# Where a split operand waits for its place: T4's slot lent to a weight, and six reloads of the output moved ahead

## The chip, the core and the metric

One core of a Trainium2 chip runs the kernel. The metric is device time in microseconds of one execution, the median of several; 902.73 us for the kernel before (three runs, 902.01 to 903.17).

## The reference, cut to what matters

The layer puts 16 learned tokens ahead of a sequence of 2048, normalises it, projects it once to eight groups of 512 columns, runs a gated short convolution on four groups and a chunked retention with four heads on the other four, and projects the concatenated result back, with a residual and a last normalisation.

```python
hn = rms_norm(h, norm_g)
proj = jnp.einsum('bld,de->ble', hn, w_in)
cx, cb, cc, cg, q, k, v, rg = jnp.split(proj, 8, axis=-1)
conv_out = short_conv_branch(cx, cb, cc, conv_w) * jax.nn.silu(cg)
qf = rotary(q.reshape(shp), pos) * (RET_HEAD_DIM ** -0.5)
kf = rotary(k.reshape(shp), pos)
ret = head_group_norm(retention_chunkwise(qf, kf, vf), ret_norm_g)
mixed = jnp.concatenate([conv_out, ret * jax.nn.silu(rg)], axis=-1)
return rms_norm(h + jnp.einsum('ble,ed->bld', mixed, w_out), final_g)
```

## The kernel before, in words

Every large product is done in single precision by three passes: `split` (L103, L111) cuts an operand into a high part (an ACT cast) and a low part (a subtraction, on VectorE by default), and TensorE multiplies low by high, high by low and high by high. An operand of 512 columns (the moving side, `mh` and `ml`) stays in a slot of its own, `mh{i}{kt}` for operand i and row block kt; `operand` (L139) gives operand 7 the slot of operand 4.

Two ways of multiplying share these operands. `quad` (L199, matmuls at L208) is Strassen and Winograd's scheme: a 2 x 2 block product by seven products instead of eight, with operands 0 to 6 of the moving side, where 0, 1 and 5 are blocks, and 2, 3, 4 and 6 the sums T2, T1, T3 and T4. `quad_plain` (L247, matmuls at L258) multiplies the four blocks themselves, operands 0, 7, 1 and 5, and needs none of the sums; its weights are split into a slot of the moving side that is not yet in use (`plain_parts`, slots `FIRST_W` and `PLAIN_W`). It is used where the sums are not there yet: twice for the first head of the first half of the rows (`r == 0`), once for the second half, once for the first pair of the output.

The rows are worked in two halves, `r`. In each, four retention heads (`head`) come first, then four convolution groups (`conv_group`). At the front of the first half `moving` loads and splits the blocks of x; `block_sums` makes the sums (T1 in `t1`, T3 in `t3`, T2 in `b22`, T4 in `b21`); T2 and T4 are split at once, and T1 and T3 in `rest()`, after the second plain quad, because `PLAIN_W` is T1's slot. For the second half and for the output weights the sums are made ahead by `prepare` and stored in DRAM (`sums_x`, `sums_w`); `prepared` loads them through tiles of the pool `g` (16 tiles of 512 columns) and splits them. In the output, `output(0, ...)` loads T2 and T4 ahead of its plain quad and T1 and T3 after it; `output(1, ...)` is the first Strassen quad there.

Of a retention head, these names matter: `kv` and `qg` hold the rotated keys, values and queries, `pm` the masked scores (VectorE, L603), read by the matmuls L611, next to L612, which read the states; L573 and L578 are transposes of keys and values, L588 the state matmuls, L601 the scores. After `pm` the output of a head is normalised over its columns (statistics L617 and L619, GpSimd's power L624, VectorE's L628) and transposed (L635).

The order in which each engine issues is set by a scheduler at build time, which simulates the program; the kernel's text gives dependencies and priorities. So an edit of the text moves instructions elsewhere. All loads and stores are issued from SP, in one queue.

Of the kernel before, what the change touches and what calls it, by code (L numbers as in the profile page):

```python
# [14 lines left out]
P = 128  # L15
# [4 lines left out]
NG = 4  # L20
# [9 lines left out]
HIGH = 400  # L30
BRIEF = 2
BLOCK = ((0, 7), (1, 5))
FIRST_W, PLAIN_W, B12 = 2, 3, 4
SUMS = (3, 2, 4, 6)


# [32 lines left out]
def hybrid_trunk(ctx: ExitStack, tc: tile.TileContext, t, out: bass.AP, chunk_decay):  # L69
# [20 lines left out]
    def gen(name="g"):  # L90
        return sb.tile([P, HB + 16], F32, name=name, tag="g", bufs=GEN)[:, : 2 + HB]
# [96 lines left out]
                nc.sync.dma_start(dst[n, kt], a)  # L188
            yield

    def prepared(m, src, ns):

        for n in ns:
            for kt in range(KH):
                a = gen("t")[:, :HB]
                nc.sync.dma_start(a, src[n, kt])
                parts(m, SUMS[n], kt, a)

    def quad(w, m, take):  # L199
# [43 lines left out]
    def plain_parts(loads, slot=PLAIN_W):  # L243
        w = {n: plain_part(n, loads[n], slot)[1] for n in (0, 2, 1, 3)}
        return [w[n] for n in range(4)]
# [398 lines left out]
    def output(pair, m, final_g):  # L644
        d = mixed[pair // 2]
        loads = [
            lambda a, i=i, k=k: nc.sync.dma_start(a.rearrange("p (k c) -> p k c", k=KH), d[pair % 2, i, k])
            for i in range(2)
            for k in range(2)
        ]  # L650
        ys = [[None, None], [None, None]]
        ss = small.tile([P, 2, 2], F32, name="so", tag="so")
        for i in range(2):
            for j in range(2):
                y = gen("yo")[:, :HB]
                row = (2 * pair + i) * P
                nc.sync.dma_start(y, x[row : row + P, j * HB : (j + 1) * HB])
                ys[i][j] = y
        last = [None]

        def take(i, j, pp, c):
            y = ys[i][j]
            if c is not None:
                add(nc.gpsimd, y, y, c)
            last[0] = nc.vector.tensor_tensor(out=y, in0=pp, in1=y, op=ALU.add)  # L665
            junk = sb.tile([P, HB], F32, name="rot", tag="rot", bufs=1)
            nc.scalar.activation(junk, y, AF.Square, accum_out=ss[:, i, j : j + 1])
            if i == j:
                ys[i][j] = gen("z")[:, :HB]
                nc.gpsimd.tensor_tensor(out=ys[i][j], in0=y, in1=final_g[:, j * HB : (j + 1) * HB], op=ALU.mult)  # L670

        if pair == 0:
            w = plain_parts(loads)
            prepared(m, sums_w, (1, 3))
            quad_plain(w, m, take)
            prepared(m, sums_w, (0, 2))
        else:
            quad(stationary(load_raw(loads)), m, take)
        for i in range(2):
            tot = small.tile([P, 1], F32, name="tot", tag="tot")  # L680
            add(nc.vector, tot, ss[:, i, 0:1], ss[:, i, 1:2])
            rs = small.tile([P, 1], F32, name="rf", tag="rf")
            rsqrt_mean(rs, tot)
            row = (2 * pair + i) * P
            for j in range(2):
                cs = slice(j * HB, (j + 1) * HB)
                y = ys[i][j]
                if i == j:
                    nc.scalar.mul(y, y, rs)
                else:  # L690
                    with tc.issue_after(last[0].ins):
                        nc.vector.scalar_tensor_tensor(
                            out=y, in0=y, scalar=rs, in1=final_g[:, cs], op0=ALU.mult, op1=ALU.mult
                        )
                nc.sync.dma_start(out[row : row + P, cs], y)
# [24 lines left out]
    warm_up(WARM)  # L720
    nc.sync.dma_start(gain, t["norm1_g"])
    factors = [[] for _ in range(NR)]
    for r in range(NR):
        f = factors[r]
        rot_t = sb.tile([P, 2, BLK], F32, name="rot_t", tag="rot_t", bufs=1)
        p0 = NMETA + r * BLK

        def load_tables():
            nc.sync.dma_start(rot_t, t["rot"][:, :, p0 : p0 + BLK])

        if r == 0:
            w = [None] * 4
            loads = w_loads(0)

            def begin(half):
                for n in (half, 2 + half):
                    w[n] = plain_part(n, loads[n], FIRST_W)

            m, b = moving(
                load_x(r), gain_of, {(0, 0): lambda: begin(0), (0, KH - 1): lambda: begin(1), (0, KT - 1): normalise_meta}  # L740
            )
            first = [[p for a, p in w]]
            blocks = None, meta_products([a for a, p in w])
            first.append(plain_parts(w_loads(1)))
            load_tables()
            nc.sync.dma_start(cols, t["cols"])
            t3 = [a[:, i * HB : (i + 1) * HB] for a in (row_tile("t3") for _ in range(2)) for i in range(2)]
            t1 = [brief("t1") if n < BRIEF else sb.tile([P, HB], F32, name="t1", tag="tc", bufs=COPIES) for n in range(KH)]
            for kt in range(KH):
                b11, b21, b12, b22 = (b[n * KH + kt] for n in range(4))  # L750
                block_sums(b11, b12, b22, b21, t1[kt], t3[kt], gain_of(kt), gain_of(KH + kt), nc.gpsimd)
                parts(m, 2, kt, b22)
                parts(m, 6, kt, b21)
            for _ in row_factors(0, f):
                pass
            nc.sync.dma_start(causal, t["causal"])
            nc.sync.dma_start(conv_w, t["conv_w"])
            nc.sync.dma_start(ret_g, t["ret_norm_g"])

            def rest():  # L760
                for i, held in ((3, t1), (4, t3)):
                    for kt in range(KH):
                        parts(m, i, kt, held[kt])

            between = (lambda: None, rest)
            later = prepare(load_x(1), sums_x, gain_of)
        else:
            m, b = moving(load_x(r), gain_of)
            first = [plain_parts(w_loads(0))]
            load_tables()  # L770
            prepared(m, sums_x, (1, 3))
            between = (lambda: prepared(m, sums_x, (0, 2)),)
            blocks = None, None
            later = prepare(load_w_out, sums_w)
        for h in range(NG):
            blocks = head(h, r, m, rot_t, f, blocks, lambda: ahead(r, h + 1), *((first, between) if h == 0 else ()))
            if h > 0:
                next(later, None)
                next(later, None)
        steps = row_factors(r + 1, factors[r + 1]) if r < NR - 1 else iter(())  # L780
        for g in range(NG):
            blocks = conv_group(g, r, m, f, blocks, lambda: ahead(r, NG + g + 1))
            for _ in range(3):
                next(steps, None)
# [44 lines left out]
```

## Time and profile before

| what | value |
|---|---|
| median of three runs | 902.73 us (902.01 to 903.17) |
| the profiled execution | 903.85 us |
| its span on the core | 902.1 us |
| mean granted TensorE clock | 0.994 |
| TensorE busy | 885.0 us, 98% |
| VectorE busy | 714.6 us, 79% |
| ACT busy | 406.1 us, 45% |
| GpSimd busy | 398.9 us, 44% |
| DMA | 116.94 MB, mean 130 GB/s |

The page is of one execution. Its span leaves out 1.75 us around the program's instructions. A TensorE that is busy for 98% need not be at its pace: matmuls overlap, and their ends are modelled, so the distance from start to start tells more than the busy time. The clock is given as a share of 2.4 GHz; 0.50 is 1.2 GHz.

### The profile page before, as it was taken

The page shows a single profiled execution, that of the slowest core. Times are in us where ns is not written, and L with a number is a line of the kernel's source. Part 1 is how long each engine was busy: PE and PEld are TensorE (multiplying, and loading weights), DVE is VectorE, ACT ScalarE, POOL GpSimd, SP SyncE. Part 2 cuts the span into 40 slices and gives each one's busy share as a digit, 9 for nine tenths or more (in the row PEclk, how much of TensorE's full clock was granted, in tenths as well). Part 3 has the DMA queues.
Part 4 walks back from the last instruction along what each step waited for, and adds up shares of the span by engine and source line. Part 5 has one row for each costly group of instructions (what it writes and reads, how often), then busy time and mean ns, then how long its engine had stood idle before and what let it go on. Part 6 is the DMA issues. An engine that isn't in the chain of part 4 may idle for free.

```text
span 902.1 us, 12862 instructions
## 1 busy us (share of the span) xinstructions
PE 885.0 (98%) x4407; PEld 727.8 (81%) x4407; DVE 714.6 (79%) x1173; ACT 406.1 (45%) x815; POOL 398.9 (44%) x294
## 2 busy tenths in 40 slices
PE   8998999999999999999999999999999999999996
PEld 5787888888878777788888888888888878788885
DVE  6798888897686776899889899777667697866764
ACT  8771342424344443655333332433333465554553
POOL 0533132323355554461333323345546445777763
PEclk9998999999999999999999999999999999999999
DMA  9711352623234232744125262113231685555532
GB/s 333 239 40 38 104 195 59 205 82 107 79 103 127 78 108 78 253 180 141 38 73 203 73 236 68 50 56 90 57 88 48 210 280 178 162 186 152 182 111 93
DMA packets 76242, 116.94 MB, mean 130 GB/s; under 512 B 7632, under 2 KB 24336, under 8 KB 76176
## 3 DMA queue, kind: packets, MB, share of 16 engines
q1 hardware_dynamic: 76176, 116.11, 40.1%
q8 instruction: 35, 0.57, 0.3%
q14 instruction: 31, 0.25, 0.1%
HBM read 90.92 MB, written 25.17 MB: 129 GB/s over the span
## 4 chain that ended last, share of the span: by engine, by line
PE 83%; DVE 9%; DMA 3%; ACT 2%; issue 2%; POOL 1%; SPq 0%; POOLq 0%; DVEq 0%; ACTq 0%
PE pj L208 66%; PE pj L258 7%; DVE ml L111 2%; DVE wl L111 2%; PE ms L611 2%; PE ms L612 1%; PE ms L601 1%; PE ms L588 1%; PE ms L392 1%; DVE rot L513 1%; DMA ra<-in_w_in 1%; PE ms L635 1%; PE ms L573 1%; DVE rot L512 1%; PE ms L578 1%
## 5 line engine op out<-in xcount | busy, mean ns | idle before, releaser
L208 PE MATMUL pj<-mh,wl 128*128 128x512 f32 x1008 | 400.0, 397 | 1.0 <-ACT tc L215 0.8
L208 PE MATMUL pj<-ml,wh 128*128 128x512 f32 x1008 | 394.2, 391 | 1.1 <-DVE ml L111 1.1
L208 PE MATMUL pj<-mh,wh 128*128 128x512 f32 x1008 | 393.4, 390 | 0.0
L99 ACT CAST wh<-ra 128x512 fp32r<-128x512 f32 x216 | 133.8, 620 | 315.1 <-PE pj L208 272.4
L208 PEld LDWEIGHTS pj<-mh,wl 128*128 128x128 f32 x1008 | 189.6, 188 | 43.1 <-ACT tc L215 2.2
L208 PEld LDWEIGHTS pj<-ml,wh 128*128 128x128 f32 x1008 | 189.8, 188 | 39.6 <-DVE ml L111 1.9
L208 PEld LDWEIGHTS pj<-mh,wh 128*128 128x128 f32 x1008 | 189.6, 188 | 39.8
L111 DVE TENSOR_TENSOR wl<-ra,wh 128x512 fp32r<-128x512 f32 x216 | 192.4, 892 | 36.2 <-ACT wh L99 35.2
L111 POOL TENSOR_TENSOR ra<-ra 128x512 f32<-128x512 f32 x72 | 113.0, 1570 | 82.0 <-DVE qg L556 32.3
L108 POOL TENSOR_TENSOR sa<-ra 128x512 f32<-128x512 f32 x36 | 54.9, 1525 | 122.6 <-DVE wl L111 62.1
L111 POOL TENSOR_TENSOR ra<-sa,ra 128x512 f32<-128x512 f32 x36 | 52.2, 1450 | 98.3 <-DVE wl L111 98.0
L215 ACT COPY tc<-pj 128x512 f32<-128x512 f32 x108 | 62.6, 580 | 0.0
L258 PE MATMUL pj<-ml,mh 128*128 128x512 f32 x128 | 50.8, 396 | 0.1
L258 PE MATMUL pj<-mh,mh 128*128 128x512 f32 x128 | 50.2, 395 | 0.0
L258 PE MATMUL pj<-mh,ml 128*128 128x512 f32 x128 | 48.5, 396 | 1.5 <-DVE ml L111 1.5
L624 POOL TENSOR_TENSOR rp<-rs,neg_half 128x4 f32<-128x4 f32 x16 | 19.9, 1245 | 51.0 <-DVE rs L108 50.8
L466 POOL TENSOR_TENSOR c<-c,rr 128x512 f32<-128x512 f32 x16 | 30.0, 1874 | 24.0 <-DVE c L454 13.6
L108 DVE TENSOR_TENSOR tc<-pj,tc 128x512 f32<-128x512 f32 x32 | 22.0, 688 | 23.4 <-PE pj L208 23.4
L111 DVE TENSOR_TENSOR ml<-t,mh 128x512 fp32r<-128x512 f32 x40 | 36.6, 961 | 0.8 <-ACT mh L99 0.8
L99 ACT CAST wh<-sa 128x512 fp32r<-128x512 f32 x36 | 22.3, 620 | 32.7 <-PE pj L208 32.7
L665 DVE TENSOR_TENSOR yo<-pj,yo 128x512 f32<-128x512 f32 x32 | 22.0, 688 | 18.8 <-POOL yo L108 8.9
L466 POOL TENSOR_TENSOR c<-c,tc 128x512 f32<-128x512 f32 x16 | 27.3, 1706 | 19.0 <-ACT tc L492 17.6
(128 smaller groups left out, 1134.3 us busy)
## 6 DMA issues: line engine op xcount, KB each, us to landing
ra<-in_w_in SPq DMA_DIRECT2D x128, 256.0 KB, 2.7
x<-in_xT SPq DMA_DIRECT2D x48, 256.0 KB, 5.1
w<-in_w_out SPq DMA_DIRECT2D x32, 256.0 KB, 5.0
ra<-mixed SPq DMA_DIRECT2D x32, 256.0 KB, 2.7
yo<-in_x SPq DMA_DIRECT2D x32, 256.0 KB, 4.4
ra<-in_x SPq DMA_DIRECT2D x16, 256.0 KB, 3.7
mixed<-qg SPq DMA_DIRECT2D x16, 256.0 KB, 2.3
sums_x<-x SPq DMA_DIRECT2D x16, 256.0 KB, 2.4
```

The costliest lines, as they stand in the source:

```text
L99: nc.scalar.copy(out=hi, in_=src)
L108: eng.tensor_tensor(out=out, in0=a, in1=b, op=ALU.add)
L111: eng.tensor_tensor(out=out, in0=a, in1=b, op=ALU.subtract)
L208: nc.tensor.matmul(bank, a[:, ks], b, start=first and kt == 0 and n == 0, stop=kt == KH - 1 and n == 2, skip_group_check=not first,)
L215: nc.scalar.copy(out=c, in_=bank)
L258: nc.tensor.matmul(banks[i], a[:, ks], b, start=half + kt + n == 0, stop=half == 1 and kt == KH - 1 and n == 2,)
L392: nc.tensor.matmul(four[i], meta_s[:, i % 2 * KH + kt, :], blocks[i][:, kt * P : (kt + 1) * P], start=kt == 0, stop=kt == KH - 1,)
L466: eng.tensor_tensor(out=out, in0=a, in1=b, op=ALU.mult)
L512: nc.vector.tensor_tensor(out=rot[:h, :w], in0=a[h:], in1=table[h:, 1, :], op=ALU.mult)
L611: nc.tensor.matmul(o[:, cs], pm[:, cs], vt[j][:, cs], start=True, stop=False)
L624: nc.gpsimd.tensor_tensor(out=rp, in0=rs, in1=neg_half.rearrange("p (c a) -> p c a", a=1), op=ALU.pow)
L665: last[0] = nc.vector.tensor_tensor(out=y, in0=pp, in1=y, op=ALU.add)
```

## The change

Three things. The second plain quad's weights go to T4's slot (`SECOND_W = 6`) instead of T1's; so T1 is split together with T2, and T4, which needs the lent slot, in `rest()` with T3. In the last convolution group of the second half six loads are added, T1's four blocks and two of T3's, from `sums_w` into tiles that are idle by then: the rotation table's tile `rot_t` (four blocks) and a tile of the pool that held the row factors (two). The output's `prepared(m, sums_w, (0, 2))` takes these six as they are, and loads the other two.

```diff
-FIRST_W, PLAIN_W, B12 = 2, 3, 4
+FIRST_W, SECOND_W, PLAIN_W, B12 = 2, 6, 3, 4
...
-    def prepared(m, src, ns):
+    def prepared(m, src, ns, held={}):
 
         for n in ns:
             for kt in range(KH):
-                a = gen("t")[:, :HB]
-                nc.sync.dma_start(a, src[n, kt])
+                a = held.get((n, kt))
+                if a is None:
+                    a = gen("t")[:, :HB]
+                    nc.sync.dma_start(a, src[n, kt])
                 parts(m, SUMS[n], kt, a)
...
-            prepared(m, sums_w, (0, 2))
+            prepared(m, sums_w, (0, 2), held)
...
-            first.append(plain_parts(w_loads(1)))
+            first.append(plain_parts(w_loads(1), SECOND_W))
...
                 parts(m, 2, kt, b22)
-                parts(m, 6, kt, b21)
+                parts(m, 3, kt, t1[kt])
...
-                for i, held in ((3, t1), (4, t3)):
+                for i, held in ((4, t3), (6, b[KH : 2 * KH])):
                     for kt in range(KH):
                         parts(m, i, kt, held[kt])
...
+            if r == NR - 1 and g == NG - 1:
+                idle = sb.tile([P, 2, BLK], F32, name="held", tag="rot_t", bufs=1), row_tile("held")
+                places = [a[:, i * HB : (i + 1) * HB] for a in (idle[0][:, 0], idle[0][:, 1], idle[1]) for i in range(2)]
+                for n, kt in [(0, kt) for kt in range(KH)] + [(2, 0), (2, 1)]:
+                    held[n, kt] = places.pop(0)
+                    nc.sync.dma_start(held[n, kt], sums_w[n, kt])
```

How the built order moves is best seen where TensorE reads `pm` of the first head. In the kernel before, VectorE's queue around that instruction (`wl` is the low part of a product's stationary operand, `rot` and `kv` a rotation, `state` an update of the states):

```order
L591 SCALAR_TENSOR_TENSOR state_785<-state_783,ms_774 128x128
L111 TENSOR_TENSOR wl_925<-ra_730,wh_924 128x512
L512 TENSOR_TENSOR rot_962<-kv_960,rot_t_112 64x512
L513 TENSOR_TENSOR rot_962<-kv_960,rot_t_112 64x512
L514 TENSOR_TENSOR kv_960<-kv_960,rot_t_112 128x512
L591 SCALAR_TENSOR_TENSOR state_808<-state_785,ms_803 128x128
L108 TENSOR_TENSOR kv_960<-kv_960,rot_962 128x512
L591 SCALAR_TENSOR_TENSOR state_810<-state_808,ms_803 128x128
L603 SCALAR_TENSOR_TENSOR pm_821<-ms_816,cols_74,causal_77 128x512
L591 SCALAR_TENSOR_TENSOR state_812<-state_810,ms_803 128x128
```

and with the change (the lines of the code are two further down):

```order
L593 SCALAR_TENSOR_TENSOR state_783<-state_781,ms_774 128x128
L516 TENSOR_TENSOR kv_960<-kv_960,rot_t_112 128x512
L111 TENSOR_TENSOR wl_929<-ra_734,wh_928 128x512
L593 SCALAR_TENSOR_TENSOR state_785<-state_783,ms_774 128x128
L108 TENSOR_TENSOR kv_960<-kv_960,rot_962 128x512
L108 TENSOR_TENSOR kv_1008<-pj_932,tc_994 128x512
L111 TENSOR_TENSOR wl_1053<-ra_1043,wh_1052 128x512
L605 SCALAR_TENSOR_TENSOR pm_821<-ms_816,cols_74,causal_77 128x512
L593 SCALAR_TENSOR_TENSOR state_808<-state_785,ms_803 128x128
```

`wl_929`, the sum `kv_1008` from a bank and `wl_1053`, a weight of the next quad, now stand ahead of `pm`, and two of the states behind it.

On TensorE, at the first matmul that reads `pm` (in `mh43_713`, 4 is the operand and 3 the row block). Before:

```order
L208 MATMUL pj_932<-ml43_714,wh_920 128x512
L208 MATMUL pj_932<-mh43_713,wh_920 128x512
L611 MATMUL ms_823<-kv_504,pm_821 128x128
L612 MATMUL ms_823<-state0_82,qg_615 128x128
L611 MATMUL ms_823<-kv_504,pm_821 128x128
L612 MATMUL ms_823<-state_779,qg_615 128x128
```

With the change:

```order
L210 MATMUL pj_932<-ml63_714,wh_928 128x512
L210 MATMUL pj_932<-mh63_713,wh_928 128x512
L613 MATMUL ms_823<-kv_504,pm_821 128x128
L614 MATMUL ms_823<-state0_82,qg_615 128x128
L613 MATMUL ms_823<-kv_504,pm_821 128x128
L614 MATMUL ms_823<-state_779,qg_615 128x128
```

Before, those matmuls come right after the product with operand 4, the fifth; now after the one with operand 6, the seventh, so 24 matmuls (12 with operand 5, 12 with operand 6) have passed ahead of them. The transposes of the first half's keys and values, which stood ahead of the quad's first product, now stand behind its second.

In the output, VectorE's queue at the end of the plain quad. Before (`yo` are the output's tiles, `t` the reloaded sums, 3 is T1 and 4 is T3):

```order
L665 TENSOR_TENSOR yo_7121<-pj_7198,yo_7121 128x512
L665 TENSOR_TENSOR yo_7119<-pj_7255,yo_7119 128x512
L665 TENSOR_TENSOR yo_7123<-pj_7256,yo_7123 128x512
L108 TENSOR_TENSOR tot_7361<-so_7116 128x1
L271 TENSOR_SCALAR rs_v_7364<-tot_7361 128x1
L108 TENSOR_TENSOR tot_7371<-so_7116 128x1
L271 TENSOR_SCALAR rs_v_7374<-tot_7371 128x1
L692 SCALAR_TENSOR_TENSOR yo_7119<-yo_7119,rf_7363,final_g_7114 128x512
L692 SCALAR_TENSOR_TENSOR yo_7121<-yo_7121,rf_7373,final_g_7114 128x512
L111 TENSOR_TENSOR wl_7416<-sa_7398,wh_7415 128x512
L111 TENSOR_TENSOR ml30_7316<-t_7313,mh30_7315 128x512
L111 TENSOR_TENSOR ml31_7322<-t_7319,mh31_7321 128x512
```

With the change:

```order
L667 TENSOR_TENSOR yo_7129<-pj_7206,yo_7129 128x512
L111 TENSOR_TENSOR ml40_7338<-held_6725,mh40_7337 128x512
L111 TENSOR_TENSOR ml41_7342<-held_6725,mh41_7341 128x512
L111 TENSOR_TENSOR ml30_7322<-held_6724,mh30_7321 128x512
L111 TENSOR_TENSOR ml32_7330<-held_6724,mh32_7329 128x512
L667 TENSOR_TENSOR yo_7127<-pj_7263,yo_7127 128x512
L667 TENSOR_TENSOR yo_7131<-pj_7264,yo_7131 128x512
L111 TENSOR_TENSOR ml31_7326<-held_6724,mh31_7325 128x512
L111 TENSOR_TENSOR ml33_7334<-held_6724,mh33_7333 128x512
L108 TENSOR_TENSOR tot_7357<-so_7124 128x1
L108 TENSOR_TENSOR tot_7367<-so_7124 128x1
```

Four splits of the six held blocks now stand between the plain quad's first and last sums, two right behind these, and the last two of T3 behind the sum tile's weight split.

## Rows read from the trace of the kernel before

**Rows 1.** Page, parts 1 and 2: TensorE busy; its granted clock in forty slices.

```profile
PE 885.0 (98%) x4407; PEld 727.8 (81%) x4407; DVE 714.6 (79%) x1173; ACT 406.1 (45%) x815; POOL 398.9 (44%) x294
...
PEclk9998999999999999999999999999999999999999
```

**Rows 2.** Chain in order of time: start us, us, what.

```profile
777.69 117.27 PE pj L208 x516
```

**Rows 3.** Waits of TensorE: us in total, times, longest us.

```profile
PE ms L611 <- DVE pm L603: 3.7, 1, 3.7
...
PE pj L208 <- DVE ml L111: 1.1, 2, 0.7
```

**Rows 4.** Windows: length, busy (x) of PE, PEld, DVE, ACT, POOL, PEclk, DMA.

```profile
76.00:79.80 3.80, 0.06 (x1) 0.00 (x0) 3.75 (x8) 0.62 (x1) 0.00 (x0) 0.86 0.25 69
...
79.80:85.40 5.60, 5.59 (x21) 5.21 (x22) 3.48 (x14) 0.00 (x0) 1.89 (x3) 0.50 0.12 47
...
729.50:732.00 2.50, 1.33 (x6) 0.80 (x5) 2.50 (x4) 2.24 (x5) 0.22 (x1) 1.00 0.81 261
```

**Rows 5.** Timeline of TensorE, first head: start us, us, instruction [idle before <- releaser].

```profile
63.88 1.05 PE L588 MATMUL ms<-kv,kd 128*128 128x128 f32 x8
...
65.82 0.48 PE L208 MATMUL pj<-mh,wl 128*128 128x512 f32 x1
...
79.81 0.79 PE L611 MATMUL ms<-kv,pm 128*128 128x128 f32 x2 [3.75 <-DVE pm L603]
...
83.24 0.77 PE L208 MATMUL pj<-mh,wl 128*128 128x512 f32 x1
```

**Rows 6.** Timeline of VectorE, first head.

```profile
50.35 3.69 DVE L111 TENSOR_TENSOR ml<-t,mh 128x512 fp32r<-128x512 f32 x6
...
58.23 1.68 DVE L513 TENSOR_TENSOR rot<-kv,rot_t 64x512 f32<-64x512 f32 x1
...
59.95 3.37 DVE L111 TENSOR_TENSOR ml<-t,mh 128x512 fp32r<-128x512 f32 x2
...
64.85 0.67 DVE L111 TENSOR_TENSOR wl<-ra,wh 128x512 fp32r<-128x512 f32 x1
...
79.01 0.74 DVE L603 SCALAR_TENSOR_TENSOR pm<-ms,cols,causal 128x512 f32<-128x512 f32 x1
...
83.62 0.89 DVE L617 BATCH_NORM_STATS2 st<-ms 128x6 f32<-128x128 f32 x4 [1.68 <-PE ms L612]
...
86.12 1.37 DVE L628 TENSOR_SCALAR pm<-ms,mv,rp 128x128 f32<-128x128 f32 x4 [1.13 <-POOL rp L624]
```

**Rows 7.** Timeline of GpSimd, first head.

```profile
57.66 1.71 POOL L111 TENSOR_TENSOR ra<-ra 128x512 f32<-128x512 f32 x1 [8.90 <-PE ms L392]
```

**Rows 8.** Timeline of TensorE, the output's first Strassen quad.

```profile
769.54 0.39 PE L208 MATMUL pj<-mh,wh 128*128 128x512 f32 x1
...
770.09 0.50 PE L208 MATMUL pj<-mh,wl 128*128 128x512 f32 x1 [0.15 <-ACT tc L215]
...
771.00 0.50 PE L208 MATMUL pj<-ml,wh 128*128 128x512 f32 x1 [0.41 <-DVE ml L111]
...
771.58 0.40 PE L208 MATMUL pj<-mh,wl 128*128 128x512 f32 x1
...
772.69 0.50 PE L208 MATMUL pj<-ml,wh 128*128 128x512 f32 x1 [0.71 <-DVE ml L111]
```

**Rows 9.** Timeline of VectorE, the output.

```profile
758.38 1.37 DVE L665 TENSOR_TENSOR yo<-pj,yo 128x512 f32<-128x512 f32 x2 [3.44 <-PE pj L258]
...
765.42 3.24 DVE L111 TENSOR_TENSOR ml<-t,mh 128x512 fp32r<-128x512 f32 x3 [0.78 <-ACT mh L99]
...
769.18 4.66 DVE L111 TENSOR_TENSOR ml<-t,mh 128x512 fp32r<-128x512 f32 x4
```

**Rows 10.** SP's queue, second half of the rows; DMA issues: count, KB, us to landing.

```profile
491.81 3.85 SPq L188 DMA_DIRECT2D sums_w<-w  x3
...
sums_w<-w SPq DMA_DIRECT2D x16, 256.0 KB, 2.1
```

More of the change, by code (lines that the diff above doesn't have):

```diff
@@ L722, in hybrid_trunk @@
     factors = [[] for _ in range(NR)]
+    held = {}
     for r in range(NR):
```

## The prediction

> **What bounds the kernel now.** I read the page first: TensorE counts as busy for 885.0 of 902.1 us, and its granted clock is below nine tenths in one slice of forty only, the fourth, 68 to 90 us [rows 1]. So the bound is TensorE, and what a change can give is the time in which it stands or runs slowly. The chain in order of time gives its pace: 516 products follow each other in 117.27 us, 0.2273 us each, with no pause among them [rows 2]; a start-to-start distance above that is loss. Next the waits of TensorE alone: one of 3.7 us for the masked score tile `pm` of the first head, and short ones for `ml`, the low halves of split operands [rows 3]. The windows show what the first costs beyond itself: in 76.0 to 79.8 us TensorE does nothing while VectorE works for 3.75 of 3.80 us, and the next 5.6 us run at a granted clock of 0.50, the 1.2 GHz level [rows 4]. The idle 3.75 us end at 79.81 us, with the matmuls that read `pm` [rows 5]. VectorE is why: from 54 to 79.75 us it goes through its queue with hardly a pause, and `pm` stands at the end of it [rows 6]. The second place is the output: five starts in 769.54 to 772.69 us, which should be 0.23 us apart where they follow each other, are 0.55, 0.91 and 1.11 us apart at three points [rows 8].
>
> So there is 3.75 + 5.6 x 0.5 = 6.55 us to be had at the first head, and 0.32 + 0.68 + 0.88 = 1.9 us at the output.
>
> **The front: T1 earlier, T4 later.** No instruction is added or removed: four splits of T1 and four of T4 change places, each one ACT cast and one VectorE subtraction at some 0.6 us (six of them in 3.69 us, [rows 6]). Two of T1's now run near 20 us, 1.2 us of VectorE work in a queue that is full there; what they push back are the splits of the first quad's last operands, which TensorE reads several products later, and the pauses of VectorE before 36 us take them up, as T4's two are gone there. I cost this at nothing; if the cover is gone it is 1.2 us. Up to the end of the six splits at 50.35 + 3.69 = 54.04 us [rows 6] the two queues hold the same number of splits, so VectorE stands there at the same time as before.
>
> What counts is the order that comes out of it, in the two pieces on `pm`. On TensorE the products with the weights' sixth and seventh stationary operands (24 matmuls) now stand ahead of the matmuls that read `pm`. That is 24 x 0.2273 = 5.45 us of cover: TensorE ran out of work at 79.81 - 3.75 = 76.06 us and would now do so at 81.5 us. On VectorE three more instructions of 512 columns stand ahead of `pm` (two weight splits and one sum from a bank) and two small state updates fewer; 3 x 0.6 = 1.8 us, the updates counted at nothing. `pm` ended at 79.01 + 0.74 = 79.75 us and would end at 81.55. The two times meet, and the 3.75 us go; with them go the 5.6 us at half clock, since nothing else idles that long.
>
> What is late next: the third product needs a weight split that ended at 64.85 + 0.67 = 65.5 us [rows 6] and now comes two instructions (1.2 us) sooner, at 64.3. TensorE began that product at 65.82 us; the state matmuls and the second head half's transposes ahead of it, from 63.88 on [rows 5], now come after it, so it is there at 63.9: a wait of 0.4 us. The seventh product needs the last weight split, which ends three instructions of 0.6, an update of 0.2 and `pm`'s 0.74 before 81.55, at 78.8 us; TensorE is there at 76.06 + 0.4 + 2.73 = 79.2: no wait. The `pm` matmuls took 3.43 us at the low clock, 79.81 to 83.24 [rows 5], and take half, so TensorE is through with them at about 83.65 and with the 24 products behind them at 89.1. There it needs the first of four normalised pieces. From the first statistic to the normalisation VectorE took 83.62 to 86.12, and a quarter of 1.37 us more for the first piece [rows 6], 2.85 us in all; this now starts behind four small updates and seven instructions after `pm`, some 5.2 us, at 86.75, and the piece is there at 89.6: a wait of 0.5 us. The bounds of these new waits together are 0 and 2.5 us. Gain of the front: 6.55 - 0.4 - 0.5 = 5.65 us.
>
> **One rule beside it.** While GpSimd runs the first of three subtractions, 57.66 to 59.37 us [rows 7], a rotation of VectorE takes 1.68 us, and beside the next ones two splits take 3.37 us, where their like take 0.6 to 0.7 [rows 6]. The Trainium skill (SBUF — State Buffer, Who interferes with whom) calls this an exclusive lock: a VectorE instruction with two SBUF inputs and a GpSimd instruction that reads SBUF block one another for a whole instruction. By it the two weight splits now ahead of `pm` could each be blocked, the sum from a bank not. I leave GpSimd's part of the 25 us as it was, because its instructions there are the same; the case in which it is not stands among the rivals, priced from the rows: 1.68 - 0.6 = 1.08 us for each instruction held.
>
> **The output.** Six of the sixteen reloads come from tiles that are filled long before. Their casts and splits move ahead: four of them into the 3.44 us in which VectorE waits for TensorE up to 758.38 [rows 9] (4 x 0.6 = 2.4 us, so they fit), because the slots they go to are free when the plain quad is in its last half; two right behind it. Between 763.95 and 773.8 us VectorE then has two splits instead of eight, of which seven took 3.24 + 4.66 us [rows 9]. The three gaps of 1.9 us hang on those splits, and go. The next wait is for the weight split from the sum tile, at 764.0 as before, and TensorE now takes eight products of T1 there before the third product: up to 0.4 us. I take a gain of 1.6 us; bounds 0.5 and 2.2.
>
> **The queues.** The six loads are issued from SP in the second half: two within the writes of the sums near 492 us, four behind the last head's rotation. There are as many transfers as before. Each is one more instruction of some 0.4 us in a queue that waits most of the time; cost nothing, unless one waits for a write (below).
>
> Sum: 5.65 + 1.6 = 7.25 us. The profiled execution took 903.85 us, 1.12 us above the median of the runs, 902.73; from 903.85 to 896.6, and for the median 902.73 - 7.25 = **895.5 us**. No change is what lies within 0.2%, 1.8 us, about what a measurement of this kernel can tell.
>
> **The rivals.**
> 1. GpSimd's instructions hold more of VectorE's, as in the two long rows of [rows 6]. Held at both weight splits and half the time at a rotation, `pm` comes 2.7 us later and TensorE waits so long. For it: the two late splits in [rows 6]. Against it: GpSimd has no more to do there. A stretch of 2.5 us with 1.17 us of idle in it left the clock at 1.00 [rows 4], so I add nothing for the clock: 902.73 - 7.25 + 2.7 = 898.2 us.
> 2. The wait is not removed but moved, to the transposes or the seventh product, is over 3 us long in one piece, and the clock falls to 1.2 GHz again as it did in [rows 4]. For it: VectorE is full for 25 us and its order is a plan, not a measurement. Then the front gives about 0.7 us: 902.73 - 1.6 - 0.7 = 900.4 us.
> 3. Slower: SP stops. A load ahead reads what a write of the same queue has just stored, and a write takes 2.1 us to land [rows 10]. If SP reaches each of the first two loads before the write has landed, it stands 2.1 us twice, with the loaded final gain (512 KB, an estimate of 4.6 us, some twice a write) between them, and the weights behind it come up to 8.8 us late, into a stretch where VectorE and TensorE are close; with 2.8 us of low clock, 902.73 - 7.25 + 11.6 = 907.1 us. It decides from where the lateness exceeds what the weight tiles were early. Against it: other writes and weight loads, which SP issued over 3.85 us [rows 10], stand between.
> 4. The order changes but TensorE's waits are made up by others of the same length: 902.7 us.
>
> **How the numbers follow.** Forecast 0.63 (893.6 to 898.2 by its bounds: all of 6.55 + 2.2 and 0.4 for small pauses, down to new waits of 2.5 us and an output gain of 0.5); first rival 0.16; second 0.12; third 0.06; fourth 0.03. The range of 893.6 to 900.2 takes in the forecast, the first rival and nearly half of the second. Faster by over 0.2% (below 900.9): 0.63 + 0.16 + 0.07 of the second = 0.86; the same 0.05 + 0.03 = 0.08; slower 0.06.
>
> **What would show it.** Right: no wait of TensorE for `pm` over 1 us, a granted clock of 1.00 from 40 to 880 us, no start-to-start gap over 0.5 us in the output's first Strassen quad, and VectorE busy in the 3.4 us before the plain quad's end. Wrong: a window at 0.50 anywhere after 10 us, a wait for `wl` or `pm` of over 2 us near 78 to 90 us, or TensorE waiting for `ra` near 500 us.

## The result, and the profile after

| kernel | median, us | runs | lowest to highest |
|---|---|---|---|
| before | 902.76 | 17 | 901.72 to 903.99 |
| changed | 905.89 | 17 | 902.93 to 907.37 |

The ratio is 1.0032, with a 95% interval of 1.0023 to 1.0041: the change made the kernel slower by about 3 us, where 7.25 us of gain were forecast. The profiled execution of the changed kernel took 906.61 us, that of the kernel before 903.85. Of the executions timed for the experiments below, two of run 4 took 2.3 and 5.1 ms and are left out.

The page first: TensorE's busy time and granted clock, to be read against [rows 1].

```profile
PE 883.1 (98%) x4407; PEld 726.1 (80%) x4407; DVE 716.5 (79%) x1173; ACT 406.3 (45%) x815; POOL 395.8 (44%) x294
...
PEclk9999999999999999999999999999999999999999
```

The dent in the fourth slice is gone, and still the span grew. The page can't say why; the waits of TensorE can (us in total, times, longest us).

```profile
PE pj L210 <- ACT tc L217: 3.2, 2, 2.4
PE pj L260 <- DVE ml L111: 2.6, 2, 1.4
PE pj L210 <- ACT kv L584: 2.3, 2, 1.5
...
PE ms L613 <- DVE pm L605: 2.0, 1, 2.0
PE pj L210 <- DVE kv L108: 1.1, 1, 1.1
PE ms L637 <- DVE pm L630: 0.9, 2, 0.7
```

In [rows 3] one wait of 3.7 us stood out; now none is over 2.43 us, and there are more of them. Where they lie is shown by TensorE's timeline.

```profile
66.28 0.47 PE L210 MATMUL pj<-mh,wl 128*128 128x512 f32 x1 [1.50 <-ACT kv L584]
...
82.10 0.50 PE L210 MATMUL pj<-mh,wl 128*128 128x512 f32 x1 [1.12 <-DVE kv L108]
...
93.01 0.33 PE L637 MATMUL ms<-ident,pm 128*128 128x128 f32 x1 [0.65 <-DVE pm L630]
...
121.14 0.47 PE L210 MATMUL pj<-mh,wl 128*128 128x512 f32 x1 [0.82 <-ACT kv L584]
...
133.31 0.49 PE L613 MATMUL ms<-kv,pm 128*128 128x128 f32 x2 [1.97 <-DVE pm L605]
...
773.35 0.50 PE L210 MATMUL pj<-mh,wl 128*128 128x512 f32 x1 [2.43 <-ACT tc L217]
```

The first three are in the first head, the next two in the second head, the last in the output's first Strassen quad. Not shown are the two for `ml` at L260: 1.38 us at 8.6 us, in the kernel before 0.29, so that this execution is 0.8 us late by the 100th matmul, and 1.17 us near 732 us, which both kernels have. The first five sum to 6.06 us; the kernel before lost 6.55 us there, waiting and at half clock together. Counting matmuls in both traces shows the same: the 500th starts 1.6 us earlier than before, the 600th 2.7 us earlier, the 700th, just behind the wait at 133.31, 0.4 us later. What the first head gave, the second took. From the 700th to the 3500th the two kernels take the same time within 0.7 us; most of the 2.8 us between these two executions arise at the output, from the 3800th to the 3900th matmul (27.2 us, before 25.3).

The windows of the changed kernel (length, busy (x) of PE, PEld, DVE, ACT, POOL, PEclk, DMA): the two of [rows 4], the second head, and the output.

```profile
76.00:79.80 3.80, 3.80 (x27) 3.44 (x26) 3.71 (x8) 0.62 (x1) 0.00 (x0) 1.00 0.15 57
79.80:85.40 5.60, 4.48 (x22) 3.44 (x21) 5.50 (x13) 0.86 (x2) 1.29 (x1) 1.00 0.20 47
...
113.00:133.30 20.30, 17.52 (x93) 14.57 (x91) 19.98 (x32) 11.02 (x26) 6.94 (x5) 1.00 0.60 195
...
774.00:777.40 3.40, 3.40 (x10) 2.63 (x9) 1.22 (x1) 0.30 (x1) 2.36 (x2) 0.50 0.60 154
```

The kernel before, in the third of these stretches:

```profile
113.00:133.30 20.30, 20.30 (x128) 17.00 (x127) 17.26 (x29) 10.83 (x26) 7.92 (x5) 1.00 0.58 207
```

So the clock stays up at the first head, as forecast, but in the second head VectorE, busy for 17.26 of 20.30 us before, is busy for 19.98 and TensorE waits for it. At the output a low stretch of 3.4 us has appeared where there was none.

VectorE at the front, changed kernel:

```profile
56.19 0.69 DVE L514 TENSOR_TENSOR rot<-kv,rot_t 64x512 f32<-64x512 f32 x1
...
60.14 1.78 DVE L108 TENSOR_TENSOR kv<-kv,rot 128x512 f32<-128x512 f32 x1
61.84 1.78 DVE L111 TENSOR_TENSOR ml<-x,mh 128x512 fp32r<-128x512 f32 x1
...
65.46 0.67 DVE L111 TENSOR_TENSOR wl<-ra,wh 128x512 fp32r<-128x512 f32 x1
...
81.36 0.68 DVE L108 TENSOR_TENSOR kv<-pj,tc 128x512 f32<-128x512 f32 x1
...
82.56 0.74 DVE L605 SCALAR_TENSOR_TENSOR pm<-ms,cols,causal 128x512 f32<-128x512 f32 x1
...
104.28 0.35 DVE L417 TENSOR_TENSOR mk<-mk,mr 16x64 f32<-16x64 f32 x2 [2.47 <-DMA mr<-in_rot_m]
...
125.61 1.74 DVE L514 TENSOR_TENSOR rot<-kv,rot_t 64x512 f32<-64x512 f32 x1
127.36 1.67 DVE L515 TENSOR_TENSOR rot<-kv,rot_t 64x512 f32<-64x512 f32 x1
...
132.51 0.74 DVE L605 SCALAR_TENSOR_TENSOR pm<-ms,cols,causal 128x512 f32<-128x512 f32 x1
```

The first rotation starts at 56.19 us; it was to follow the splits at 54.04 [rows 6]. From there to the second head's `pm` eleven VectorE instructions of 512 columns take over 0.95 us, in the kernel before nine; what they take beyond 0.69 us each sums to 9.4 us, before to 7.5. VectorE's pauses in that stretch sum to 4.1 us; none of them ends with work of TensorE, and the longest, 2.47 us at 104.28 us, is for the load of a small rotation table (`mr`). In the kernel before they sum to 9.4 us, half of that ends with work of TensorE, and none is for a load.

ACT, then VectorE, at the output's first Strassen quad:

```profile
765.84 0.61 ACT L99 CAST wh<-ra 128x512 fp32r<-128x512 f32 x1
771.58 0.63 ACT L669 ACTIVATE rot<-yo 128x512 f32<-128x512 f32 x1 [5.12 <-DVE yo L667]
...
772.21 0.60 ACT L99 CAST wh<-ra 128x512 fp32r<-128x512 f32 x1
772.72 0.58 ACT L217 COPY tc<-pj 128x512 f32<-128x512 f32 x1
```

```profile
765.71 3.48 DVE L111 TENSOR_TENSOR ml<-t,mh 128x512 fp32r<-128x512 f32 x2
769.11 1.77 DVE L111 TENSOR_TENSOR wl<-ra,wh 128x512 fp32r<-128x512 f32 x1
770.81 0.68 DVE L667 TENSOR_TENSOR yo<-pj,yo 128x512 f32<-128x512 f32 x1
```

The copy that TensorE waits for (772.72) stands in ACT's queue behind a square (771.58) that waits 5.12 us for VectorE's sum `yo` (770.81), and that one behind three splits of 1.7 us each. The Trainium skill (TensorE: Matmul & The Clock Gate, Architectural detail) says that ACT and VectorE take their instructions strictly in order; the trace agrees, for the cast and the copy behind the square start only when it is done. Not all of the 5.12 us is lost by that: in run 3, where the square stands behind them, ACT waits 3.60 us for TensorE at this place, and TensorE's own wait is 0.29 us instead of 2.43.

### The profile page after: what moved, and what is told of

Read it like the earlier page. It is cut to its first block, busy times and chain, and to the rows that moved or that the text cites. A ratio compares the mean times of both kernels' runs of the same rounds, so it can differ in the third digit from the quotient of the medians.

```text
span 904.7 us, 12871 instructions
## 1 busy us (share of the span) xinstructions
PE 883.1 (98%) x4407; PEld 726.1 (80%) x4407; DVE 716.5 (79%) x1173; ACT 406.3 (45%) x815; POOL 395.8 (44%) x294
## 5 line engine op out<-in xcount | busy, mean ns | idle before, releaser
L111 DVE TENSOR_TENSOR wl<-ra,wh 128x512 fp32r<-128x512 f32 x216 | 196.9, 913 | 42.1 <-ACT wh L99 41.3
L260 PE MATMUL pj<-ml,mh 128*128 128x512 f32 x128 | 50.7, 396 | 0.1
L260 PE MATMUL pj<-mh,ml 128*128 128x512 f32 x128 | 48.0, 394 | 2.6 <-DVE ml L111 2.6
L260 PE MATMUL pj<-mh,mh 128*128 128x512 f32 x128 | 50.1, 394 | 0.0
L667 DVE TENSOR_TENSOR yo<-pj,yo 128x512 f32<-128x512 f32 x32 | 22.0, 688 | 20.4 <-PE pj L210 13.7
L630 DVE TENSOR_SCALAR pm<-ms,mv,rp 128x128 f32<-128x128 f32 x64 | 21.9, 404 | 15.4 <-POOL rp L626 15.4
L468 POOL TENSOR_TENSOR c<-c,tc 128x512 f32<-128x512 f32 x16 | 25.2, 1574 | 19.2 <-ACT tc L494 17.9
```

Of the source, the lines that this page charges most:

```text
L111: eng.tensor_tensor(out=out, in0=a, in1=b, op=ALU.subtract)
L260: nc.tensor.matmul(banks[i], a[:, ks], b, start=half + kt + n == 0, stop=half == 1 and kt == KH - 1 and n == 2,)
L468: eng.tensor_tensor(out=out, in0=a, in1=b, op=ALU.mult)
L630: nc.vector.tensor_scalar(out=y[:, cs], in0=o[:, cs], scalar1=mv[:, c, 0:1], scalar2=rp[:, c, :], op0=ALU.subtract, op1=ALU.mult,)
```

## The experiments

Each was timed beside the kernel before on the same chip (its medians there: 902.41 for the first four, 902.58 for the next four, 902.49 for the last three). Behind the median stand its ratio to the kernel before and, in brackets, the ratio's 95% interval. Lines of code are those of each kernel, a few further down than in the changed one.

### 1. The front alone

```diff
...
-                for n, kt in [(0, kt) for kt in range(KH)] + [(2, 0), (2, 1)]:
-                    held[n, kt] = places.pop(0)
-                    nc.sync.dma_start(held[n, kt], sums_w[n, kt])
```

> The change without its six loads ahead: T1 and T4 change places at the front, the output is as in the kernel before. My theory (the two parts lose apart: the front gives its gain back within the first two heads, and most of the loss is at the output): TensorE's waits at 8 to 135 us as in the changed kernel (for pm of the second head about 2 us, no clock below 1.00 there), none over 1.2 us at the output, 902.3 to 903.8 us. Rival (the front alone makes it slower): 905 us or more.

Measured 905.69 us, 1.0041 [1.0025, 1.0057]: the rival. My theory that most of the loss is at the output fell. The places were right, though. TensorE's waits:

```profile
PE pj L210 <- ACT kv L584: 2.2, 2, 1.5
PE ms L613 <- DVE pm L605: 1.9, 1, 1.9
```

The profiled execution took 904.08 us, at a mean clock of 0.998, the other six 903.39 to 907.18: those at 0.999 or 0.998 took 903.4 and 904.1, those at 0.994 took 906.3 to 907.2. In the profiled one the clock fell only at its end. The kernel before ran at 0.998 in three of thirty, in 899.0 to 899.8 us. So at a like mean clock the new front is some 4 us slower. The two traces differ by 0.2 us alone (904.08 and 903.85), because the one of the kernel before is 1.4 us above its median here and that of run 1 is 1.6 us below its own. An estimate of what the traces leave out: a stretch of 3.41 us at half clock, as run 3 shows one, costs 1.7 us and takes 0.0019 off the mean clock of 902 us, so that 0.994 in place of 0.998 is two such stretches, 3.4 us. By that the new front loses by its waits, and in most executions by falls of the clock too; no trace of such an execution was kept, so the falls are not shown.

### 2. The loads ahead alone

```diff
-FIRST_W, SECOND_W, PLAIN_W, B12 = 2, 6, 3, 4
+FIRST_W, SECOND_W, PLAIN_W, B12 = 2, 3, 3, 4
...
-                parts(m, 3, kt, t1[kt])
+                parts(m, 6, kt, b21)
...
-                for i, held in ((4, t3), (6, b[KH : 2 * KH])):
+                for i, held in ((3, t1), (4, t3)):
```

> The six loads ahead alone, the front as in the kernel before. My theory: the wait of 3.7 us for pm with its 1.2 GHz stretch is back, and at the output's first Strassen quad TensorE waits about 2.4 us for a copy out of its bank, with a second stretch at 1.2 GHz behind it; 904.7 to 906.5 us. Rival (the loads ahead do what they were meant to, and the output's loss in the changed kernel comes from the front's other timing): 900.8 to 901.5 us.

Measured 902.91 us, 1.0013 [1.0002, 1.0023], between the two. TensorE waits as the theory said:

```profile
770.83 0.50 PE L210 MATMUL pj<-mh,wl 128*128 128x512 f32 x1 [2.43 <-ACT tc L217]
```

and the clock fell behind it, but against the 1.9 us of [rows 8] that are gone this costs little: 0.5 us by the medians, 1.2 by the ratio.

### 3. The squares behind the copies

```diff
+            if pair == 1:
+                squares.append(square)
+            else:
+                square()
...
+            quad(stationary(load_raw(loads)), m, take, copies)
+            for square in squares:
+                with tc.issue_after(copies[2].ins):
+                    square()
```

(`copies` collects the quad's copies, `square` is the activation at L669 as a function.)

> The changed kernel with one thing more: in the output's first Strassen quad the squares of ACT are issued behind the quad's third copy. In the built order one square changes places with a weight cast and two copies, and nothing else moves on any engine. My theory (a square that waits for VectorE stands in ACT's queue ahead of the copy that TensorE waits for): the wait of 2.4 us and the 3.4 us at half clock go, 905.9 - 2.4 - 1.7 = 901.8 us, from 901.3 to 902.5. Rival (VectorE's splits, held up by GpSimd, are late themselves, and TensorE next waits for a low weight instead): 904 us or more.

Measured 903.13 us, 1.0008 [0.9994, 1.0022]: 2.8 us under the changed kernel by the medians, 2.2 by the ratios, and between theory and rival. The wait at the output shrinks from 2.43 us to this:

```profile
771.85 0.50 PE L210 MATMUL pj<-mh,wl 128*128 128x512 f32 x1 [0.29 <-ACT tc L217]
```

So the order in ACT's queue was the cause there: the order of all other instructions in the two traces is the same. The run by itself does not tell the 2.8 us from what the clock does elsewhere; runs 2 and 5, which differ by the same move, give 2.2 us by the medians and 3.2 by the ratios. A part of the expected gain is missing, and in the profiled execution the clock fell at another place, behind a wait of 1.87 us for the second head's `pm`:

```profile
133.50:136.80 3.30, 3.30 (x13) 2.91 (x12) 2.07 (x11) 0.00 (x0) 1.55 (x2) 0.50 0.23 79
```

This kernel is the base of the runs from 5 on.

### 4. T1 behind the weights

```diff
+                with tc.issue_after(weights.ins):
+                    parts(m, 3, kt, t1[kt])
```

(`weights` is the last low part of the second plain quad's weights; base: the changed kernel.)

> The changed kernel with the low parts of T1 issued behind those of the second plain quad's weights on VectorE. My theory (two splits of T1 ahead of the weights free the weights' tiles later, so the rows for the squares are loaded later and VectorE then stands 2.3 us longer for the row sums): VectorE's rotation of the first keys starts at 54 to 54.8 us instead of 56.2, the two waits of 1.5 and 1.1 us near 66 and 82 us fall under 0.5 us each, pm of the second head comes 1.5 to 2 us earlier, 903.5 to 904.5 us. Rival (VectorE's start is set by the first loads, which landed 0.8 us later in that execution): rotation at 55.5 us or later, 905.2 us or more.

Measured 903.95 us (the median of its other ten executions), 1.0025 [1.0011, 1.0039]: in the range, for other reasons. The rotation starts earlier, though later than the theory had it,

```profile
55.20 0.69 DVE L516 TENSOR_TENSOR rot<-kv,rot_t 64x512 f32<-64x512 f32 x1
```

and the wait near 82 us fell to 0.57, but the wait near 66 us grew to 1.99 us, and that for the second head's `pm` stayed at 1.95. T1's place among the first splits is not what these two hang on. Why the rotation is 1 to 2 us later than before stays open; 0.8 us of it in the changed kernel is that execution's late start, for in run 1 the rotation starts at 55.39.

### 5. The front as before, the squares behind the copies

The edits of 2 and 3 together.

> The loads ahead with the squares issued behind the copies, and the front as in the kernel before (T1 and T4 not changed places). Theory (the front is what costs: short waits of VectorE's making, more of them than the one that went; the loads ahead gain about 1.5 us once ACT's order is mended): the wait for pm of 3.7 us and its 1.2 GHz stretch as before, no wait over 0.5 us at the output; 902.9 of the loads alone less 2.4, so 899.8 to 901.2 us. Rival (the front costs nothing by itself and the runs before this differ by chance): as the same kernel with the new front, 902.4 us or more.

Measured 900.69 us, 0.9978 [0.9969, 0.9987], as the theory said: the loads ahead are worth 1.9 us once ACT's queue is in order, and with them in place the front costs 903.13 - 900.69 = 2.4 us (run 3 less this one; 2.7 by the ratios). Of the 2.8 us between the two traces 1.7 are there at the 1000th matmul; most of the rest is a wait of 0.75 us near 690 us, of which run 9 tells more. The old wait is there, 3.8 us for `pm`.

### 6. The sums one head later

```diff
-            if h > 0:
+            if h > (1 if r == 0 else 0):
                 next(later, None)
```

> The changed kernel with the squares behind the copies, and the sums of the second half's operands prepared from the third head on instead of the second: six scaled sums of 0.74 us and two subtractions of 0.6 leave VectorE's queue ahead of the second head's pm, 5.7 us. Theory (with TensorE's long wait gone, VectorE is the bound from 55 us to that pm): the waits of 0.7 us near 120 and 1.9 us near 132 go, TensorE is 2 to 2.6 us earlier at 136 us, and the clock does not fall there; 900 to 901.2 us against 903.1. Rival (those waits come from somewhere else, as a load or the order in the first head): 902.6 us or more.

Measured 897.71 us, 0.9945 [0.9932, 0.9957], 5.4 us under the base and more than expected. Between the traces of runs 3 and 6 lie 6.2 us: 4.2 are there at the 1000th matmul, of which 1.7 is run 3's low stretch, and 2.1 more come near 690 and 733 us (see run 9). The second head's window, with VectorE free for 2.6 of 20.4 us, has no wait of TensorE:

```profile
113.00:133.40 20.40, 20.40 (x116) 17.76 (x115) 17.83 (x36) 9.85 (x24) 8.33 (x8) 1.00 0.22 65
```

The waits of the first head are still there (2.0, 1.2 and 0.6 us). VectorE's queue up to the second `pm` is what took the front's gain. The edit also moves the loads of these sums (the DMA share of the stretch falls from 0.60 in the changed kernel to 0.22); run 8, which leaves the sums where they are, also has shorter waits there.

### 7. The first sums on VectorE

```diff
-            quad(stationary(blocks[0]), m, take)
+            quad(stationary(blocks[0], nc.vector if r == 0 and h == 1 else nc.gpsimd), m, take)
```

(`stationary` makes its four sums on the engine that it is given.)

> The changed kernel with the squares behind the copies, and the four sums of the second head's first weights on VectorE instead of GpSimd. VectorE has 4 x 0.6 = 2.4 us more to do, and loses three instructions of 1.6 to 1.8 us at 58 to 63 us (0.7 each alone) and one of 1.25 near 49 us (0.15 alone). Theory (GpSimd's subtractions hold VectorE's instructions, and this is a part of what the front costs): none of VectorE's instructions of 512 columns between 45 and 66 us takes over 1.0 us, VectorE is 1 to 2 us earlier at 66 us, TensorE's waits near 65 and 81 us sum to under 1.8 us instead of 2.8; 901.5 to 902.7 us. Rival (it is VectorE's number of instructions that counts): waits of 4 us or more there, 904 us or more.

Measured 901.25 us, 0.9988 [0.9979, 0.9996]: the theory, and a little better. With more instructions VectorE is earlier at the third product's weight split (63.81 us, in run 3 64.64), for none of them is held up between 48 and 67 us:

```profile
58.87 0.68 DVE L111 TENSOR_TENSOR ra<-ra 128x512 f32<-128x512 f32 x1
59.47 0.69 DVE L111 TENSOR_TENSOR ml<-x,mh 128x512 fp32r<-128x512 f32 x1
...
60.48 0.67 DVE L108 TENSOR_TENSOR kv<-kv,rot 128x512 f32<-128x512 f32 x1
```

The sum at 60.48 took 1.78 us in the changed kernel, beside GpSimd's subtraction. The rule of an exclusive lock (the Trainium skill, SBUF — State Buffer, Who interferes with whom) holds here with its price: 1.0 to 1.1 us for each instruction held. TensorE's waits near 65 and 81 us shrink to one of 0.77 us. But the second head has new ones, and the clock fell there, which I had not expected:

```profile
117.03 0.49 PE L592 MATMUL ms<-kv,kd 128*128 128x128 f32 x2 [1.60 <-ACT kv L586]
118.60 0.69 PE L577 MATMUL ms<-ident,kv 128*128 128x128 f32 x2 [1.09 <-DVE qg L640]
```

```profile
118.30:121.60 3.30, 3.00 (x14) 3.00 (x15) 3.27 (x7) 2.67 (x7) 0.72 (x1) 0.50 0.85 297
```

### 8. The table in a tile of its own

```diff
-        rot = sb.tile([P, HB], F32, name="mr", tag="tc", bufs=COPIES)[:NMETA, : 2 * P].rearrange("p (a c) -> p a c", a=2)
+        rot = small.tile([P, 2 * P], F32, name="mr", tag="mr", bufs=1)[:NMETA].rearrange("p (a c) -> p a c", a=2)
```

> The changed kernel with the squares behind the copies, and the rotation table of the 16 learned tokens in a tile of its own, so that its load does not stand behind weight loads in SP's queue. Theory (VectorE's one idle stretch ahead of the second head, 2.4 us for that table at 101 to 103.4 us, is what TensorE later waits for): that idle time goes, the waits near 120 and 132 us, 2.6 us together, fall under 1 us; 901 to 902 us. Rival (VectorE catches up nothing, because its next work waits for TensorE anyway): waits as before, 902.8 us or more.

Measured 900.79 us, 0.9983 [0.9975, 0.9992]: the theory. The idle 2.4 us of VectorE at 101 us are gone, near 120 us there is no wait, and that for the second head's `pm` is 0.7 us. How much of the 2.3 us against run 3 this is worth is less plain: of the 3.6 us between the traces 2.0 are there at the 1000th matmul, and 2.2 come near 690 and 733 us (see run 9), with 0.5 lost between. Here the clock fell in the first head:

```profile
65.11 0.47 PE L210 MATMUL pj<-mh,wl 128*128 128x512 f32 x1 [1.81 <-DVE wl L111]
```

```profile
66.30:69.60 3.30, 3.30 (x9) 2.55 (x9) 3.27 (x6) 0.00 (x0) 1.84 (x1) 0.50 0.25 83
```

### 9. The sums later, with the front as before

The edits of 2, 3 and 6 together.

> The sums one head later, as in the run before, but with the front as in the kernel before (loads ahead and squares behind the copies kept). Theory (VectorE is the bound up to the second head's pm only where TensorE has its 3.7 us back; in the old front TensorE does not wait there): the wait of 3.7 us for the first pm and its 1.2 GHz stretch stay, nothing else changes, 900.0 to 901.0 us against 900.7; so the new front is worth 3 us once VectorE's queue is shorter. Rival (the sums later are worth 3 us in any front, and the new front nothing): 897.5 to 898.5 us.

Measured 898.90 us, 0.9962 [0.9949, 0.9974], between the two. With runs 3, 5 and 6 this makes a square:

| | sums as built | sums one head later |
|---|---|---|
| front as before | 900.69 | 898.90 |
| new front | 903.13 | 897.71 |

The new front costs 2.4 us where VectorE has the sums to do in the second head, and gains 1.2 where it has not; that last figure is about as large as what the two intervals leave open, the 3.6 us between the two differences are not. The traces say the same: the 1000th matmul starts at 187.7 and 186.4 us in the upper row, at 189.4 and 185.2 in the lower, so the new front costs 1.7 us in one column and gains 1.3 in the other. That the sums later also help the old front by 1.8 us I had not expected. The wait for the first `pm` is as long as ever, 3.75 us, but the low stretch behind it is half as long as the 6.83 us of runs 2 and 5, beginning at 80.5 us:

```profile
80.50:83.90 3.40, 3.40 (x13) 2.92 (x12) 2.17 (x11) 0.00 (x0) 1.93 (x3) 0.50 0.21 77
```

Whether the edit shortened it or chance did is open. By the 1000th matmul 1.3 of the 2.3 us between the traces of runs 5 and 9 are there. The rest is a wait of 1.16 us for `ml` at 730 us that run 5 has and run 9 has not. VectorE, then GpSimd there, in run 5:

```profile
727.16 1.78 DVE L111 TENSOR_TENSOR wl<-ra,wh 128x512 fp32r<-128x512 f32 x1
...
726.98 1.41 POOL L470 TENSOR_TENSOR c<-c,tc 128x512 f32<-128x512 f32 x1 [3.89 <-ACT tc L496]
```

and in run 9:

```profile
725.88 0.68 DVE L111 TENSOR_TENSOR wl<-ra,wh 128x512 fp32r<-128x512 f32 x1
...
725.69 5.03 POOL L470 TENSOR_TENSOR c<-c,tc 128x512 f32<-128x512 f32 x1 [3.90 <-ACT tc L496]
```

In the one VectorE's split is the longer by 1.1 us, in the other GpSimd's sum by 3.6. The order of instructions in this part is the same in the two kernels, and in runs 2 to 11 but for the square, and still the traces of runs 3, 4, 5 and 11 have the wait and the others not; a wait of 0.75 us near 690 us comes and goes likewise. So 1 to 2 us between two traces can arise in a part that the edit did not touch; what decides it is open.

### 10. The sums later, the first sums on VectorE

The edits of 6 and 7 together.

> The changed kernel with the squares behind the copies, the sums one head later, and the four sums of the second head's first weights on VectorE. Theory: TensorE's waits of 2.0, 1.2 and 0.6 us near 66, 82 and 93 us sum to under 1.8 us instead of 3.8, and the waits near 117 to 124 us, which this placing of the sums had by itself, go with the shorter queue; 895.0 to 896.6 us. Rival (the two reliefs share what they give): 897 us or more.

Measured 897.67 us, 0.9945 [0.9931, 0.9958]: the rival. The first head is 2.9 us faster than in run 6 (the 500th matmul), the second gives all but 0.1 us of it back (the 700th), in waits for ACT and VectorE:

```profile
116.49 0.49 PE L592 MATMUL ms<-kv,kd 128*128 128x128 f32 x2 [1.59 <-ACT kv L586]
...
119.58 0.50 PE L210 MATMUL pj<-mh,wl 128*128 128x512 f32 x1 [1.06 <-DVE wl L111]
```

### 11. All three

The edits of 6, 7 and 8 together.

> The same with the rotation table in a tile of its own. Theory: VectorE's queue ahead of the second head's pm is no bound any more, so the table's 2.4 us of idle time are worth nothing further: within 0.7 us of the run before. Rival (still VectorE): 1.5 to 2.5 us faster.

Measured 901.62 us, 0.9993 [0.9983, 1.0003]: neither. Its order is another one, in which a product of the second head comes too early for its weight:

```profile
121.58 0.50 PE L210 MATMUL pj<-mh,wl 128*128 128x512 f32 x1 [2.52 <-DVE wl L111]
```

Reliefs that help apart don't add up where a planner orders the work anew. Runs 6 and 10 are the fastest, 0.55% under the kernel before; run 6 is the smaller edit.

## Why the prediction was wrong, point by point

**The first head.** The mechanism was right: no wait for the first `pm`, a clock of 1.00 at 76 to 85 us, the 24 products as cover. `pm` was forecast to end at 81.55 and ended at 82.56 + 0.74 = 83.3 us. The new waits were mis-sized: 0.4 us forecast at the third product, 1.50 measured, because its weight split ended at 65.46 + 0.67 = 66.1 us instead of 64.3 (the profile names a copy of ACT, L584, that ended 0.1 us later; in runs 3, 4 and 6 it names the split); none at the seventh product, 1.12 measured; 0.5 at the normalised pieces, 0.65 measured. The first is VectorE's late start (56.19 for 54.04, with the 0.8 us by which this execution began late), which I had costed at nothing on the ground that "the two queues hold the same number of splits". The second was in my own times: the seventh product writes the bank that the sum `kv_1008` reads, and by the working that sum ends 0.74 + 0.6 us ahead of 81.55, at 80.2, an end that I did not hold against TensorE's 79.2. Bounds of 0 to 2.5 us for these waits together did not hold their 3.3 us.

**What is late next.** This is the step that failed. I followed VectorE's queue to the first head's transposes and stopped. But it goes on to the second head's `pm` without once waiting for TensorE, and TensorE, 2.7 us earlier by then, met it there: 0.82 + 1.97 us. The sum of 5.65 us held a gain that no later wait had been held against; at the 700th matmul TensorE was 0.4 us late. In the kernel before, the 3.75 us and the slow 5.6 us also gave VectorE time to catch up. In the new order VectorE comes to the rotation table before its load has landed and stands 2.47 us, where before it did not wait for it; I had not looked at this load. Run 8 takes that pause away, and the waits of the second head fall from 2.6 to 0.7 us. Run 6 shows it from the other side: with 5.7 us of work out of that queue, the second head's waits are gone, and the front is worth a small gain, 1.2 us by run 9, where 5.65 were forecast.

**The clock.** I took 1.17 us of idle as harmless and over 3 us as harmful, with nothing between. The traces show falls behind waits of 1.6 to 2.4 us in some cases and not in others, each 3.4 us long. The new front has two waits of 1.5 to 2.0 us where the old one had a single long one. So the 5.6 x 0.5 = 2.8 us of the slow stretch, which the sum of 6.55 us booked as won, were not won for sure: the mean clock of most executions of run 1 suggests that the clock still fell.

**The first rival**, GpSimd's hold on VectorE, priced at 2.7 us and given 0.16, has something in it: 9.4 - 7.5 = 1.9 us more. Its place was wrong: 1.1 us of it lie at 113 to 129 us, in the second head. Run 7 shows that it counts.

**The second rival** had the wait moved in one piece of over 3 us. It moved in five pieces, none over 2 us, which in the traced execution sum to 6.06 us, nearly the 6.55 us of the one with its slow stretch.

**The third rival**, SP stopping at the loads, did not happen: in the trace SP issues the first two within 0.38 us each, and no wait of TensorE lies there. The fourth, waits of the same length in other places, had 0.03 and describes the front best.

**The output.** The gain of 1.6 us was right for what the splits cost: 1.9 us in run 5. What failed is that the order was read for VectorE alone. The same scheduler put a square of ACT ahead of the copy that TensorE needs; it costs a wait of 2.43 us, where up to 0.4 was forecast, and a chance of a low stretch, and run 3 shows it by moving that one instruction.

## What to carry to other kernels

When a wait of the bounding engine is taken away, follow the engine it waited for to the next place where the two meet, and further, until that engine waits for the bounding one again: up to there the gain is only lent. The pauses in which VectorE waited here for a load or for GpSimd gave nothing back. In a queue that a planner orders, read every engine's order around the edit, and look for an instruction that waits for a slow engine ahead of one that the bounding engine needs. And price several short waits by what the clock does behind them, not by their sum.

## What the runs showed of the hardware that was not expected

TensorE's clock fell to 0.50 behind idle times much shorter than the 3.75 us of [rows 4]: behind 2.43 us at 773 us (changed kernel) and in run 2, behind 1.87 us (run 3), 1.81 us (run 8), and 1.60 us with a further 1.09 us close behind (run 7), for 3.4 us each time. It did not fall behind 2.52 us (run 11), 2.41 us (run 4, at the same place of the output), 2.00 us (run 6), 1.97 us (changed kernel), 1.89 us (run 1) and 1.60 us (runs 10 and 11). Behind the wait of 3.75 us the low stretch was 6.83 us long in three traces and 3.41 us in one. The mean clock, too, differs between executions of one program. Run 1's executions spread over 3.8 us, and those with the lower mean clock took longer (903.4 us at 0.999, 906.3 to 907.2 at 0.994); run 6's, with fewer waits, spread over 1.0 us.

Of a VectorE and a GpSimd instruction side by side, either can be the one that takes longer, with the same order of instructions: near 727 us VectorE's split took 1.78 us and GpSimd's sum 1.41 in run 5, 0.68 and 5.03 us in run 9.
